# The mLSTM branch's row sums formed beside the attention branch's pairs, and three moves in the order of loads

## The chip, the cores and the metric

The kernel runs on one core of one Trainium2 chip. The metric is the device time of one execution in microseconds (us); the number to beat or miss is the median of three runs. A profiled execution gives a page and a trace, from which every duration below comes. Engines go by the names of the profile: PE is TensorE's matmul, PEld its weight load, DVE VectorE, ACT ScalarE, POOL GpSimd, SP SyncE (which issues most DMAs; SPq is its queue).

## What is computed

One layer of a hybrid decoder, for a prompt of 512 tokens and 8 samples of 4 new tokens each (544 columns, T), width 2048, all in float32:

```python
u = x @ w_in                       # q, k, v, o, z of the mLSTM; q, k, v, z of attention; two gates
h_m = mlstm(q_m, k_m, v_m, ig, lf)             # 4 heads of 512; chunked, with state C, n, m
h_a = sliding_window_attention(q_a, k_a, v_a)  # 32 heads of 64, 4 key heads, window 128, sinks
br_m = layernorm(h_m) * norm_w * sigmoid(o_m) * silu(z_m)
br_a = h_a * silu(z_a)
y = sigmoid(g_m) * (br_m @ w_proj_m) + sigmoid(g_a) * (br_a @ w_proj_a)
out = layernorm(alpha * x + y @ w_out)
```

The samples attend to a stored window of 128 keys and values each (`state_attn_k`, `state_attn_v`, 1 MB each) and update a stored mLSTM state.

## The kernel before

**Products.** Each float32 product is made of three fp32r products: an operand is split into a high part (a cast, ACT: `hilo` or `split`) and the rest (a subtraction, DVE). A *plain tile* is 128 output rows: for each of 16 blocks k of 128 inputs, three products in two halves of 272 columns, 96 matmuls of 128x272 (`gemm`, L232; `products`, L213). Its weights come in two halves (`raw`, 512 KB, by SP), each split into `wh` and `wl` of 128x1024; `wh` and `wl` have two buffers.

A *pair* (`paired`, L726) makes two output tiles with a Strassen-like scheme: seven half products of 24 matmuls instead of 192 matmuls in all. It needs sums of blocks of the activations: beside the operand itself four sums, called s1, n2, n3 and s4, which join blocks k and k+8 and the two halves of columns. Sums of the weights are formed on DVE, or by an adding DMA on POOL. A pair's weights are prepared three steps (half products) ahead.

**Stages.** First the products with `w_in`, beside which the attention runs as generators (`tick` in `products` and `paired` lets each of them go one step on); then plain tiles 0 to 5 of the attention branch's output product, beside which the four mLSTM heads run; then the two branches' products (`w_proj_a`, stage A, and `w_proj_m`, stage M), each partly in plain tiles and partly in pairs; then `w_out`.

- Stage A: eight plain tiles, three pairs, plain tiles 14 and 15. The four sums of its operand were formed earlier and stored in DRAM (`d_sa`); `stored_sums` (L1646) loads them on POOL's queue and splits them.
- Its tiles 14 and 15 run beside `branch(d_brm, ...)` (L1411), which loads the 16 blocks of the M operand on SP (`ev` and `c` buffers; `c6` has two) and splits them into `bh` and `bl`.
- Stage M: plain tiles 0 to 3, five pairs, plain tiles 14 and 15. Beside the four plain tiles runs `operand_sums` (L1616): it loads blocks k and k+8 on POOL's queue (`tx`), forms the four sums (four DVE instructions of 128x272) and splits each.

**Order.** Every engine executes its instructions in an order fixed when the kernel is built; a scheduler lays it down from the program's order, priorities (`tc.high_priority`) and ties (`tc.issue_after(x)`: not before x in the order). So an instruction that waits holds up all that stands behind it on its engine or queue.

**The samples' attention** (`sample_attention`, L953) runs late in the first stage. It loads the new keys, values and gates, then eight pieces of queries (`qraw`, L977), then the old keys (`kb`) and values (`vb`, both L982), all on SP. PE turns the old keys (L991).

**The mLSTM** (`mlstm`, L1562): for each head `decays(h)` forms a matrix `dm` of decays (one matmul, one DVE sum, ten exponentials on ACT), `values` and `keys` turn and split the operands (`kwh` is the high part of the weighted keys; L1487 multiplies with it), then `cells` does the rest.

Of the kernel before, what the change touches and what calls it, by code (L numbers as in the profile page):

```python
# [15 lines left out]
F32 = mybir.dt.float32  # L16
# [58 lines left out]
def _build(tc, nc, i, o, es):  # L75
# [106 lines left out]
    d_y = dr.tile([16, 128, T], F32, name="d_y")  # L182
    d_sa = dr.tile([8, 128, 4, SEQ - T // 2], F32, name="d_sa")
    d_ss = dr.tile([128, 4, 8, NS], F32, name="d_ss")
    d_o = dr.tile([12, 128, T], F32, name="d_o")
# [46 lines left out]
    def gemm(wv, c0, xh, xl, cols=EVEN, raws=(None, None), every=8, prio=0, before=None, parts=(1, 1),  # L232
             ps=None, behind=None):
# [12 lines left out]
        return ps  # L246
# [706 lines left out]
    def sample_attention():  # L953
# [5 lines left out]
        vas = t1.tile([32, 256], F32, name="vas")  # L959
        with tc.issue_after(state["load"].ins):  # L960
            nc.sync.dma_start(kas[:], d_ka[:, :, SEQ:T].rearrange("k p t -> p k t"))
            nc.sync.dma_start(vas[:], d_vr[SEQ:T])
            nc.sync.dma_start(gas[:], d_bra[:, :, SEQ:T].rearrange("k p t -> p k t"))
        kb = t1.tile([128, NB, 256], F32, name="kb")
# [4 lines left out]
        G.memset(En[:], 0.0)  # L969
        st = t1.tile([128, 4, NB], F32, name="sast")  # L970
        for kvh in range(KVH):
            half = slice((kvh % 2) * 64, (kvh % 2) * 64 + 64)
            if kvh % 2 == 0:
                yield
            with tc.issue_after(state["load"].ins):
                for a in range(2):
                    nc.sync.dma_start(qraw[half, kvh // 2, a::2],  # L977
                                      d_qa[kvh * 4:kvh * 4 + 4, a * 64:a * 64 + 64].rearrange("k p t -> p k t"))
        for t_, src in ((kb, i["state_attn_k"]), (vb, i["state_attn_v"])):
            yield  # L980
            with tc.issue_after(state["load"].ins):
                nc.sync.dma_start(t_[:], src.rearrange("b t k d -> t b (k d)"))  # L982
        yield
        yield
# [171 lines left out]
    def sample_prep(h, r):  # L1156
# [73 lines left out]
        for _ in range(0 if h else 2):  # L1230
            yield
        r.update(kv=load_kv(h, 0), den=den, num=num, qs=qs)

# [327 lines left out]

    def mlstm():  # L1562
        pre = {"v": load4(d_v, 0)}
        for _ in range(4):
# [80 lines left out]

    def stored_sums(to, p):  # L1646
        f, e = ([[p.tile([128, 4, 2, HT], F32R, tag="act", name=nm("sum" + n)) for _ in range(2)] for n in "hl"]
                for _ in range(2))
        to["n2"], to["s1"], to["n3"], to["s4"] = (
            (lambda q, k, t=t, j=j: t[q][k // 4][:, k % 4, j]) for t in (e, f) for j in range(2))  # L1650

        def load(n):
            t_ = two((tx.tile([128, T], F32, tag="tx", name=nm("tx")) if n % 7 < 4 else ev())[:])[:, :, 0:PC]
            j = n // 8 * 2
            G.dma_start(out=t_, in_=d_sa[n % 8][:, j:j + 2])
            return t_

        with tc.issue_after(state["head"].ins):
            ahead = [load(n) for n in range(7)]
        rim = c6t()  # L1660
        with tc.issue_after(state["load"].ins):
            nc.sync.dma_start(rim[:, 0:512], d_ss[:, 0:2].rearrange("p j k t -> p (j k t)"))

        def behind_weights(*a):
            with tc.issue_after(state["cast"].ins), tc.issue_after(state["split"].ins):
                hilo(*a)

        def columns(to_):
            src = rim[:, 0:512].rearrange("p (j k t) -> p k j t", j=2, k=8)
            for q in range(2):  # L1670
                behind_weights(src[:, q * 4:q * 4 + 4], *(t[q][:, :, :, PC:HT] for t in to_))

        for n in range(16):
            for _ in range(2 if 8 <= n < 12 else 1):
                yield
            k, t_ = n % 8, ahead.pop(0)
            to_ = e if n < 8 else f
            behind_weights(t_, *(t[k // 4][:, k % 4, :, 0:PC] for t in to_))
            if k == 4:
                columns(to_)  # L1680
                if n < 8:
                    with tc.issue_after(state["load"].ins):
                        nc.sync.dma_start(rim[:, 0:512], d_ss[:, 2:4].rearrange("p j k t -> p (j k t)"))
            if n + 7 < 16:
                ahead.append(load(n + 7))

# [31 lines left out]
    for ct in range(LEAD_A):  # L1718
        marks.append(state.get("cells"))
        with tc.issue_after(marks[ct - 1].ins) if ct > 1 and marks[ct - 1] else ExitStack():  # L1720
            plain_a(ct, every=(1, 2), prio=0 if ct else AHEAD)
    drain()
# [8 lines left out]
    SA = {}  # L1731
    sums_ = stored_sums(SA, act3)
    next(sums_)
# [10 lines left out]
    esB2.close()  # L1744
    tx = pool(esR, "txc", 2)
    bm_, bmh, bml, g_ = branch(d_brm, act3, lambda k: ev() if k % 5 < 3 else c6t(), order=(2, 3, 0, 1))
# [26 lines left out]
    drain()  # L1773
    XM = operands(bm_, M)
# [13 lines left out]

    paired([merge_pair(ct) for ct in range(4, 14, 2)], state["split"])
    state["end"] = None  # L1790
# [288 lines left out]
```

## Time and profile before

| | us |
|---|---|
| median of 3 runs (lowest, highest) | 2471.68 (2469.76, 2472.47) |
| profiled execution | 2473.6 |
| its span | 2471.8 |
| PE busy in it | 2431.3 |
| DVE, ACT, POOL busy | 1912.5, 1246.3, 526.6 |
| mean granted PE clock | 0.995 |

The span is the time from the first to the last instruction on the core; the profiled execution took 1.8 us more than its span. "Granted clock" is the share of PE's full speed that the throttle allowed. In a row of waits, `PE sm L991 <- DMA kb<-in_state_attn_k: 3.5, 1, 3.5` says that PE, at line 991 (writing a tile `sm`), waited once, for 3.5 us, for the DMA that fills `kb`. In a timeline, a row is the start, the duration, the engine, the line and what it did, and behind it in brackets the idle time before it and what ended that.

### The profile page before, as it was taken

What the parts mean: (1) busy time and instruction counts of PE and PEld (TensorE: products, weight loads), DVE (VectorE), ACT (ScalarE), POOL (GpSimd) and SP (SyncE); (2) the same over time, 40 slices, a digit from 0 to 9 for tenths busy, and PEclk for the clock granted to TensorE, in tenths of its full rate; (3) what the DMA queues carried; (4) which work ended last, traced back from release to release, by engine and by line L of the source; (5) the groups of instructions that cost most, each with busy time, mean ns of one, the idle gap of its engine ahead of it and who ended that gap; (6) DMA issues with size and microseconds to landing.
All of it is one profiled execution on the core that took longest, in us unless ns stands there. A gap on an engine that the chain in (4) does not pass through costs nothing.

```text
span 2471.8 us, 48922 instructions
## 1 busy us (share of the span) xinstructions
PE 2431.3 (98%) x19374; PEld 2374.7 (96%) x19374; DVE 1912.5 (77%) x2860; ACT 1246.3 (50%) x2064; POOL 526.6 (21%) x503
## 2 busy tenths in 40 slices
PE   9999999999999999999999999999999999999997
PEld 8999999999999998999999999999999999999997
DVE  7778888888888896887878888878755676777667
ACT  6466676676676654433433444544644444334431
POOL 4114334333334320121121122110000120110111
PEclk9999999999999999999999999999999999999998
DMA  6876666667776755578687677687754598798876
GB/s 180 201 178 158 155 163 149 161 160 164 176 178 164 172 139 135 130 229 244 183 239 241 170 235 230 178 250 216 242 165 154 177 259 255 213 228 252 214 221 193
DMA packets 568478, 479.01 MB, mean 194 GB/s; under 512 B 48313, under 2 KB 463465, under 8 KB 567993
## 3 DMA queue, kind: packets, MB, share of 16 engines
q1 hardware_dynamic: 549208, 409.30, 56.6%
q0 software_dynamic: 17840, 64.23, 13.3%
q8 instruction: 152, 2.49, 0.4%
q10 hardware_dynamic: 1200, 2.36, 0.3%
q14 instruction: 78, 0.63, 0.1%
HBM read 325.75 MB, written 100.77 MB: 173 GB/s over the span
## 4 chain that ended last, share of the span: by engine, by line
PE 85%; DMA 5%; issue 4%; DVE 3%; ACT 1%; SPq 1%; POOL 0%; DVEq 0%; POOLq 0%; ACTq 0%
PE bank L693 45%; PE bank L695 22%; PE bank L218 5%; PE sm L1487 2%; PE sm L218 1%; PE sm L1519 1%; PE sm L808 1%; PE bank L1294 1%; PE sm L1535 1%; DVE wl L209 1%; PE sm L859 1%; DMA tx<-d_brm 1%; PE sm L1945 1%; DMA VB<-d_kv 1%; PE sm L834 1%
## 5 line engine op out<-in xcount | busy, mean ns | idle before, releaser
L208 ACT CAST wh<-raw 128x1024 fp32r<-128x1024 f32 x641 | 671.6, 1048 | 819.6 <-PE bank L693 698.6
L209 DVE TENSOR_TENSOR wl<-raw,wh 128x1024 fp32r<-128x1024 f32 x641 | 800.2, 1250 | 191.0 <-ACT wh L208 164.9
L693 PE MATMUL bank<-xk,wh 128*128 128x272 f32 x2336 | 323.9, 289 | 0.0
L673 DVE TENSOR_TENSOR raw<-raw,raw 128x1024 f32<-128x1024 f32 x244 | 311.1, 1276 | 14.5 <-DMA raw<-in_w_in 8.4
L693 PEld LDWEIGHTS bank<-xk,wh 128*128 128x128 f32 x2336 | 303.4, 188 | 2.9 <-issue 2.4
L712 POOL TENSOR_TENSOR ev<-p,ev 128x272 f32<-128x272 f32 x85 | 114.4, 1346 | 483.2 <-ACT ev L711 435.4
L693 PE MATMUL bank<-n2h,wh 128*128 128x272 f32 x656 | 170.4, 292 | 2.3 <-ACT wh L208 2.3
L693 PE MATMUL bank<-s1h,wh 128*128 128x272 f32 x656 | 170.5, 292 | 0.0
L695 PE MATMUL bank<-xk,wl 128*128 128x272 f32 x1168 | 169.9, 288 | 0.0
L693 PE MATMUL bank<-n3h,wh 128*128 128x272 f32 x656 | 169.5, 291 | 0.0
L693 PE MATMUL bank<-s1l,wh 128*128 128x272 f32 x656 | 168.8, 289 | 0.0
L693 PE MATMUL bank<-n2l,wh 128*128 128x272 f32 x656 | 167.9, 287 | 0.0
L693 PE MATMUL bank<-n3l,wh 128*128 128x272 f32 x656 | 167.5, 288 | 0.0
L693 PE MATMUL bank<-s4h,wh 128*128 128x272 f32 x656 | 167.1, 288 | 0.0
L693 PE MATMUL bank<-s4l,wh 128*128 128x272 f32 x656 | 166.8, 287 | 0.0
L695 PEld LDWEIGHTS bank<-xk,wl 128*128 128x128 f32 x1168 | 155.6, 188 | 0.1
L671 POOL DMA_DIRECT2D raw<-raw x96 | 83.2, 867 | 316.6 <-DVE ev L720 200.8
L693 PE MATMUL bank<-a11h,wh 128*128 128x272 f32 x584 | 150.5, 289 | 0.0
L693 PE MATMUL bank<-a11l,wh 128*128 128x272 f32 x584 | 149.4, 288 | 0.0
L693 PEld LDWEIGHTS bank<-n2h,wh 128*128 128x128 f32 x656 | 123.5, 188 | 3.6 <-ACT wh L208 2.8
L693 PEld LDWEIGHTS bank<-s1h,wh 128*128 128x128 f32 x656 | 124.4, 190 | 1.0 <-issue 0.7
L693 PEld LDWEIGHTS bank<-n3h,wh 128*128 128x128 f32 x656 | 123.4, 188 | 1.7 <-issue 1.4
(516 smaller groups left out, 5798.5 us busy)
## 6 DMA issues: line engine op xcount, KB each, us to landing
raw<-in_w_in SPq DMA_DIRECT2D x296, 512.0 KB
raw<-raw POOLq DMA_DIRECT2D x96, 512.0 KB, 5.0
C<-in_state_mlstm_C SPq DMA_DIRECT2D x32, 1024.0 KB
out<-C SPq DMA_DIRECT2D x64, 512.0 KB
raw<-in_w_proj_a SPq DMA_DIRECT2D x32, 512.0 KB
raw<-in_w_proj_m SPq DMA_DIRECT2D x32, 512.0 KB
raw<-in_w_out SPq DMA_DIRECT2D x32, 512.0 KB
d_v<-ev SPq DMA_DIRECT2D x16, 272.0 KB
```

Of the source, the lines that this page charges most:

```text
L208: state["cast"] = A.copy(wh[:, k:k + n], raw[:, k:k + n])
L209: state["split"] = V.tensor_tensor(out=wl[:, k:k + n], in0=raw[:, k:k + n], in1=r32(wh[:, k:k + n]), op=ALU.subtract)
L218: PE.matmul(ps[f][:, :w], a[:, kk], b(k, c, w), start=(k == 0 and n == 0), stop=(k == 15 and n == 2))
L671: G.dma_start(out=w[out][:], in_=w[b][:], accum_op=ALU.add)
L673: V.tensor_tensor(out=w[out][:], in0=w[a][:], in1=w[b][:], op=ALU.add)
L693: PE.matmul(ps, wh[:, k], x(p, k), start=(first and k == 0 and p == 0), stop=False, skip_group_check=True)
L695: state["end"] = PE.matmul(ps, wl[:, k], x(0, k), start=False, stop=(k == 7), skip_group_check=True)
L712: G.tensor_tensor(out=c22, in0=p1, in1=c11, op=ALU.subtract)
L808: PE.matmul(pp[:, c0 + w0:c0 + 256], qs[a][:, j * 128:j * 128 + 128], kx[:, k0:k0 + 256 - w0], start=(n == 0), stop=(n == 1))
L834: PE.transpose(pt[:, b * 128:b * 128 + 128], s_[:, b, 128:256], ident)
L859: PE.matmul(po[:, b * 128:b * 128 + n], VA[:, b], p_[:, 2 * b:2 * b + n // 128], start=(b == 0 and m == 0), stop=(b == 3 and m == 1), skip ...
L1487: state["cells"] = PE.matmul(pp[:, 0:258], a[:, b * 128:b * 128 + 128], b_[:, b, f], start=(b == 0 and n == 0), stop=(b == 3 and n == 2))
```

## The change

Four things, of which the first two belong together:

1. *The mLSTM branch's sums are formed earlier and stored.* A new generator, `row_sums`, runs beside stage A's three pairs and its tail: for each k of 0 to 7 it loads blocks k and k+8 on POOL's queue (into `ms` and a `c6` buffer), forms the four sums with `branch_sums` on DVE, and stores them on SP into a new DRAM tile `d_sm` (128x1088, 557 KB each). Stage M then takes its sums through `stored_sums`, which now serves both branches: 16 loads of 128x544 on POOL's queue (five `tx` buffers), and 16 splits of 128x544 instead of 32 of 128x272.
2. *Stage M has two plain tiles ahead of its pairs, not four*, and six pairs, not five.
3. *The samples' old keys are loaded first* in `sample_attention`; the eight pieces of `qraw` go to POOL's queue, and the old values are loaded two steps later.
4. *Smaller moves*: the first head's `decays` start at the mLSTM's first load; a head's `keys` come before the split of the same block; `load_kv` is tied to the last weight load; and the second half of plain tile 5 of stage A is placed behind the last head's products (`hold`).

```diff
@@ gemm
-            products(ps, half, wh, wl, xh, xl, cols, every[half] if isinstance(every, tuple) else every)
+            with tc.issue_after(state["cells"].ins) if hold and half else ExitStack():
+                products(ps, half, wh, wl, xh, xl, cols, every[half] if isinstance(every, tuple) else every)
@@ sample_attention
         with tc.issue_after(state["load"].ins):
+            nc.sync.dma_start(kb[:], i["state_attn_k"].rearrange("b t k d -> t b (k d)"))
             nc.sync.dma_start(kas[:], d_ka[:, :, SEQ:T].rearrange("k p t -> p k t"))
...
-            with tc.issue_after(state["load"].ins):
-                for a in range(2):
-                    nc.sync.dma_start(qraw[half, kvh // 2, a::2],
-                                      d_qa[kvh * 4:kvh * 4 + 4, a * 64:a * 64 + 64].rearrange("k p t -> p k t"))
-        for t_, src in ((kb, i["state_attn_k"]), (vb, i["state_attn_v"])):
-            yield
-            with tc.issue_after(state["load"].ins):
-                nc.sync.dma_start(t_[:], src.rearrange("b t k d -> t b (k d)"))
-        yield
+            for a in range(2):
+                G.dma_start(out=qraw[half, kvh // 2, a::2],
+                            in_=d_qa[kvh * 4:kvh * 4 + 4, a * 64:a * 64 + 64].rearrange("k p t -> p k t"))
+            yield
+            if kvh == 1:
+                with tc.issue_after(state["load"].ins):
+                    nc.sync.dma_start(vb[:], i["state_attn_v"].rearrange("b t k d -> t b (k d)"))
@@ mlstm
+        spawn(decays(0))
         pre = {"v": load4(d_v, 0)}
...
-            spawn(decays(h))
+            if h:
+                spawn(decays(h))
...
-                two_parts(kts[c], (kh, kl))
                 n_ = keys(h, c, kts[c])
                 next(n_)
+                two_parts(kts[c], (kh, kl))
@@ new
+    def row_sums(src, dst):
+        while sums_ in live:
+            yield
+        esB2.close()
+        ms = pool(esM, "ms", 2)
+
+        def load(k):
+            t_, o_ = ms.tile([128, 4, HT], F32, tag="ms", name=nm("ms")), c6t()
+            G.dma_start(out=t_[:, 0:4:2], in_=src[k].rearrange("p (c x) -> p c x", c=2))
+            G.dma_start(out=o_[:], in_=src[k + 8])
+            return t_, o_
+
+        ahead = [load(0), load(1)]
+        for k in range(8):
+            for _ in range(2):
+                yield
+            t_, o_ = ahead.pop(0)
+            with tc.issue_after(state["split"].ins):
+                for _ in branch_sums(t_[:], o_[:, 0:HT], o_[:, HT:T], dst[k]):
+                    pass
+            if k < 6:
+                ahead.append(load(k + 2))
@@ stage A
+    esM = ExitStack()
+    spawn(row_sums(d_brm, d_sm))
     paired([pair_a(ct) for ct in range(PAIR_A, TAIL_A, 2)], state["split"], rest=sums_)
...
-    tx = pool(esR, "txc", 2)
+    tx = pool(esR, "txc", 5)
@@ stage M
-    spawn(operand_sums(d_brm, M, act))
-    for ct in range(4):
+    sums_ = stored_sums(M, act, d_sm)
+    next(sums_)
+    spawn(sums_)
+    for ct in range(2):
         merge = merged(ct, plain=True)
-        sg = merge([p_[:, :HT] for p_ in gemm(wm, ct * 128, bmh, bml, every=4, prio=AHEAD)])
+        sg = merge([p_[:, :HT] for p_ in gemm(wm, ct * 128, bmh, bml, every=2, prio=AHEAD)])
...
-    paired([merge_pair(ct) for ct in range(4, 14, 2)], state["split"])
+    paired([merge_pair(ct) for ct in range(2, 14, 2)], state["split"], rest=sums_)
```

How the change moves instructions. In what follows each block is a run of one engine's rows; the number behind a tile's name is the build's count. The lines of the changed kernel lie a little further down (L991 is L990 there, L977 stays, L218 is L219, L209 is L210, L254 is L256, L1696 is L1729).

SP's queue at the samples' attention, before:

```order
L879 DMA d_sa<-s_11208 512x1x240
L195 DMA raw_11508<-in_w_in 128x8x128
L961 DMA kas<-d_ka 128x2x32
L962 DMA vas<-d_vr 32x256
L963 DMA gas<-d_bra 128x16x32
L977 DMA qraw<-d_qa 64x4x32 x8
L982 DMA kb<-in_state_attn_k 128x8x256
L982 DMA vb<-in_state_attn_v 128x8x256
```

and in the changed kernel:

```order
L881 DMA d_sa<-s_11209 512x1x240
L196 DMA raw_11509<-in_w_in 128x8x128
L970 DMA kb<-in_state_attn_k 128x8x256
L971 DMA kas<-d_ka 128x2x32
L972 DMA vas<-d_vr 32x256
L973 DMA gas<-d_bra 128x16x32
L982 DMA vb<-in_state_attn_v 128x8x256
```

The load of `kb` has moved from behind eleven small loads to directly behind the weights.

PE at the turning of the old keys, before (`a11h` is the first half product of a pair, `s4h` the sixth):

```order
L695 MATMUL bank_11710<-a11h_114,wl_11579 128x272 x4
L991 MATMUL sm_11568<-cc,kb 128x128 x2
L991 MATMUL sm_11573<-cc,kb 128x128 x2
L695 MATMUL bank_11710<-a11h_114,wl_11579 128x272 x4
L693 MATMUL bank_11772<-s1h_648,wh_11641 128x272
```

and in the changed kernel:

```order
L697 MATMUL bank_11441<-s4h_723,wl_11504 128x272 x3
L990 MATMUL sm_11536<-cc,kb 128x128 x2
L990 MATMUL sm_11541<-cc,kb 128x128 x2
L697 MATMUL bank_11441<-s4h_723,wl_11504 128x272 x5
L695 MATMUL bank_11477<-xk_7_119,wh_11546 128x272
```

The first four transposes stand in the sixth half product of the pair before, not in the first of the next: five products' matmuls, a whole half product and twenty more earlier.

DVE at the end of stage A, around the merge of its tile 15 (L1696, L1729), before; `bl` is the M operand, `s1l` to `s4l` its sums:

```order
L254 TENSOR_TENSOR bl_24968<-c_3425_25244,bh_24967 128x544
L209 TENSOR_TENSOR wl_25276<-raw_25273,wh_25275 128x1024
L254 TENSOR_TENSOR n2l_25370<-tx_25303,n2h_25369 128x272
L254 TENSOR_TENSOR n2l_25370<-tx_25305,n2h_25369 128x272
L254 TENSOR_TENSOR bl_24968<-ev_25212,bh_24967 128x544
L254 TENSOR_TENSOR n3l_25374<-tx_25303,n3h_25373 128x272
L254 TENSOR_TENSOR n3l_25374<-tx_25305,n3h_25373 128x272
L254 TENSOR_TENSOR bl_24968<-ev_25260,bh_24967 128x544
L1696 TENSOR_TENSOR c_3410_25120<-bank_25122,c_3410_25120 128x272
L1696 TENSOR_TENSOR c_3410_25120<-bank_25123,c_3410_25120 128x272
L209 TENSOR_TENSOR wl_25334<-raw_25331,wh_25333 128x1024
```

and in the changed kernel (`ms` is the last row sum):

```order
L879 TENSOR_TENSOR ms_24878<-ms_24878 128x272
L1729 TENSOR_TENSOR c_3426_25197<-bank_25199,c_3426_25197 128x272
L1729 TENSOR_TENSOR c_3426_25197<-bank_25200,c_3426_25197 128x272
L880 TENSOR_TENSOR ms_24878<-c_3391_24879,ms_24878 128x272
L210 TENSOR_TENSOR wl_25441<-raw_25438,wh_25440 128x1024
L256 TENSOR_TENSOR bl_25047<-c_3418_25120,bh_25046 128x544
L256 TENSOR_TENSOR bl_25049<-ev_25158,bh_25048 128x544
L256 TENSOR_TENSOR bl_25049<-ev_25174,bh_25048 128x544
L256 TENSOR_TENSOR bl_25049<-ev_25190,bh_25048 128x544
L256 TENSOR_TENSOR bl_25049<-c_3422_25142,bh_25048 128x544
L256 TENSOR_TENSOR bl_25043<-c_3432_25219,bh_25042 128x544
L256 TENSOR_TENSOR suml_25346<-tx_25352,sumh_25344 128x544
```

Before, the last `bl` stood ahead of the merge of tile 15. Now thirteen of the sixteen stand behind it, the last one 24 rows further down, with eight stored sums and two `wl` among them.

SP's queue at the same place in the changed kernel (`c_3422`, `c_3433` and `c_3441` take turns in one `c6` buffer, which `c_3391`, the last row sum's second block, held before them):

```order
L1422 DMA c_3418_25120<-d_brm 128x544
L1730 DMA d_t<-c_3426_25197 128x544
L881 DMA d_sm<-ms_24878 128x1088
L1422 DMA c_3422_25142<-d_brm 128x544
L196 DMA raw_25644<-in_w_proj_m 128x8x128
L1791 DMA c_3507_25737<-d_sgm 128x544
L1422 DMA c_3432_25219<-d_brm 128x544
L1422 DMA ev_25251<-d_brm 128x544
L1422 DMA ev_25267<-d_brm 128x544
L1422 DMA ev_25289<-d_brm 128x544
L1422 DMA c_3433_25235<-d_brm 128x544
L1422 DMA c_3440_25305<-d_brm 128x544
```

Ten of the sixteen loads of the operand stand here, around the store of tile 15's result (L1730); before, all sixteen stood ahead of that store.

More of the change, by code (lines that the diff above doesn't have):

```diff
@@ L1644, in operands, with stored_sums, four @@
         return [side_by_side(tiles, 0), s1, n2, side_by_side(low, 0), n3, s4, side_by_side(low, HT)]
[L1646 to L1648 removed]
+    def stored_sums(to, p, src, rim=None, behind=None):
+        width = PC if rim else HT
+        def four():
+            return [[p.tile([128, 4, 2, HT], F32R, tag="act", name=nm("sum" + n)) for _ in range(2)] for n in "hl"]
+        f = four() if rim else None
+        e = four()
+        f = f or four()
         to["n2"], to["s1"], to["n3"], to["s4"] = (
             (lambda q, k, t=t, j=j: t[q][k // 4][:, k % 4, j]) for t in (e, f) for j in range(2))
+        turn, own = (7, 4) if rim else (5, 5)
         def load(n):
[L1653 removed]
+            t_ = two((tx.tile([128, T], F32, tag="tx", name=nm("tx")) if n % turn < own else ev())[:])[:, :, 0:width]
             j = n // 8 * 2
[L1655 removed]
+            G.dma_start(out=t_, in_=src[n % 8][:, j:j + 2])
             return t_
[L1658 to L1662, printed above, removed]
+        with tc.issue_after(behind.ins) if behind else ExitStack():
+            ahead = [load(n) for n in range(turn)]
+        if rim:
+            edge = c6t()
+            with tc.issue_after(state["load"].ins):
+                nc.sync.dma_start(edge[:, 0:512], rim[:, 0:2].rearrange("p j k t -> p (j k t)"))
         def behind_weights(*a):
@@ L1731, in _build @@
     SA = {}
-    sums_ = stored_sums(SA, act3)
+    sums_ = stored_sums(SA, act3, d_sa, d_ss, state["head"])
     next(sums_)
```

34 lines of the change are left out of this document (17 added, 17 removed).

## The prediction

> **What bounds the kernel now.** I read the page's first part, then the waits of TensorE, then the stretches of the two stages that the change touches, and last the timelines at the waits themselves. All times are in us. First the page, then the waits (engine, line, what it waited for: total, times, longest):
>
> ```profile
> PE 2431.3 (98%) x19374; PEld 2374.7 (96%) x19374; DVE 1912.5 (77%) x2860; ACT 1246.3 (50%) x2064; POOL 526.6 (21%) x503
> ```
> ```profile
> PE sm L1487 <- ACT kwh L253: 5.4, 3, 4.3
> PE sm L991 <- DMA kb<-in_state_attn_k: 3.5, 1, 3.5
> ...
> PE bank L218 <- DVE wl L209: 3.2, 3, 1.4
> PE bank L693 <- ACT wh L208: 2.3, 2, 1.7
> PE sm L336 <- DMA xr<-in_x_prompt: 2.2, 1, 2.2
> PE sm L1535 <- ACT t L1118: 0.9, 1, 0.9
> ```
> TensorE is busy for 98%: matmuls set the time, and all its waits together are some 25 us. So an edit gains only by fewer matmuls, by a wait of this list that goes, or by clock that isn't lost. The stretches (length, PE busy, weight loads, DVE, ACT, POOL, granted clock, DMA share, GB/s):
>
> ```profile
> 931.00:950.00 19.00, 15.51 (x181) 15.00 (x180) 10.50 (x14) 8.03 (x14) 2.73 (x2) 0.82 0.80 232
> ...
> 2010.00:2073.00 63.00, 63.00 (x505) 62.91 (x504) 43.12 (x57) 26.30 (x34) 7.71 (x8) 1.00 0.88 236
> 2073.00:2097.00 24.00, 24.00 (x195) 24.00 (x194) 15.01 (x25) 11.29 (x21) 1.51 (x2) 1.00 0.94 294
> 2097.00:2146.00 49.00, 46.55 (x368) 45.89 (x367) 37.44 (x73) 20.32 (x36) 6.04 (x7) 1.00 0.74 217
> 2146.00:2250.00 104.00, 104.00 (x834) 104.00 (x833) 69.78 (x92) 39.92 (x48) 13.19 (x13) 1.00 0.89 234
> ```
> Two things stand here. A matmul of 128x272 costs 104.00/834 = 0.1247 where nothing waits. And the merge stages (from 2010 on) keep the DMA engines at 0.88 to 0.94: TensorE is the bound there, and the DMA engines are close behind it.
>
> **The samples' old keys.** TensorE around 931, and what SyncE's queue issued before:
>
> ```profile
> 930.28 0.29 PE L693 MATMUL bank<-a11l,wh 128*128 128x272 f32 x1
> 930.40 0.66 PE L695 MATMUL bank<-a11h,wl 128*128 128x272 f32 x4
> 934.56 1.09 PE L991 MATMUL sm<-cc,kb 128*128 128x128 f32 x4 [3.50 <-DMA kb<-in_state_attn_k]
> 935.29 1.25 PE L695 MATMUL bank<-a11h,wl 128*128 128x272 f32 x4
> 936.35 0.43 PE L693 MATMUL bank<-s1h,wh 128*128 128x272 f32 x1
> ```
> ```profile
> 918.33 0.37 SPq L195 DMA_DIRECT2D raw<-in_w_in  x1
> ...
> 920.35 8.12 SPq L977 DMA_DIRECT2D qraw<-d_qa x8
> 928.52 0.60 SPq L982 DMA_DIRECT2D kb<-in_state_attn_k  x1
> ```
> The wait costs twice: 3.50 idle, and a clock of 0.82 over the 19 us after it, which is 0.18 x 19 = 3.4 of lost work (a matmul shows 0.43 instead of 0.29). The load of kb is late because SyncE spends 8.12 on eight small loads ahead of it; it then takes 934.56 - 928.52 = 6.0. In the new order kb stands right behind the weights of 918.33: issued at 918.8, there at 924.8, or 926.5 if the 0.5 MB of weights ahead of it come first. TensorE too comes earlier: the transposes move ahead by 5 + 24 + 20 = 49 matmuls (rest of one product, a whole one, 20 of the next), 6.1, so to 931.06 - 6.1 = 924.9. The new wait is 0 to 1.6, I take 1.0: a gain of 2.5 and of the 3.4 of clock. Ends: 0, if kb is as late as now, and 6.9. I take -5.9. The eight loads on POOL's queue (0.73 each by the row of L1655 below, 5.9 together) are wanted only for the scores behind kb; nothing is queued behind them there that TensorE needs within 8 us, so they cost 0, at most the 1.6 of a wait like the one above. The clock: waits of 2.2 (L336, though at the start) and 1.7 (L693) show no halved matmuls behind them, 3.5 and 4.3 do, so a wait of 1.0 should cost none. The Trainium skill (TensorE: Matmul & The Clock Gate, section What's actually happening) has the clock back after one busy window of about 3.4 us, which makes 1.7 of a halving; by it the gain here would be 1.7 smaller and the sum below that much higher. The row of 931 to 950 shows twice that, and I go by the row.
>
> **Decays at the first load.** The largest wait, 4.3 at L1487, is that of the first mLSTM head. ScalarE before it:
>
> ```profile
> 1772.80 0.62 ACT L253 CAST t<-t 128x512 fp32r<-128x512 f32 x1 [1.10 <-DMA t<-d_q]
> ...
> 1776.74 1.28 ACT L1507 ACT_TABLE_LOAD   x1
> ...
> 1780.20 1.86 ACT L1507 ACTIVATE dm<-f,colT 128x128 f32<-128x128 f32 x6
> 1781.97 0.60 ACT L253 CAST t<-t 128x512 fp32r<-128x512 f32 x1
> 1782.47 0.62 ACT L253 CAST kwh<-f 128x512 fp32r<-128x512 f32 x1
> ```
> ```profile
> 1783.23 0.64 PE L1487 MATMUL sm<-vh,kwh 128*128 128x258 f32 x2 [4.31 <-ACT kwh L253]
> ...
> 1785.19 0.43 PE L218 MATMUL bank<-bl,wh 128*128 128x272 f32 x1
> ...
> 1786.91 0.28 PE L218 MATMUL bank<-bh,wh 128*128 128x272 f32 x1
> ```
> ScalarE works without a break from 1773 on, and kwh comes last. The change moves the first decays' matmul and their DVE sum earlier, but in ScalarE's order the table load and all ten dm still stand directly ahead of kwh, and in the same order. So I take 0, between 0 and the whole 4.3 + 1.7 (half pace from 1783.2 to 1786.8). `hold` shifts half a plain tile behind the last head's products; the waits there are at most the 0.9 of L1535: 0, within 0.9 either way.
>
> **Fewer matmuls.** Two plain tiles (2 x 96) become one pair (7 x 24 = 168): 24 x 0.1247 = -3.0.
>
> **The sums of the mLSTM branch.** Two waits of the M stage were tied to forming them there:
>
> ```profile
> 2104.68 0.52 PE L218 MATMUL bank<-bh,wl 128*128 128x272 f32 x2 [1.39 <-DVE wl L209]
> 2117.98 0.52 PE L218 MATMUL bank<-bh,wl 128*128 128x272 f32 x2 [1.00 <-DVE wl L209]
> ```
> The weights' wl stood on DVE behind sums that waited for tx. These go: -2.4. But something else becomes late. Rows of DVE at the end of attention tile 15 (I call that moment T), one SyncE load and its use, and a run of four conversions:
>
> ```profile
> 2085.81 0.73 DVE L254 TENSOR_TENSOR bl<-ev,bh 128x544 fp32r<-128x544 f32 x1 [0.55 <-ACT bh L253]
> 2086.45 0.78 DVE L1696 TENSOR_TENSOR c<-bank,c 128x272 f32<-128x272 f32 x2
> 2087.15 1.22 DVE L209 TENSOR_TENSOR wl<-raw,wh 128x1024 fp32r<-128x1024 f32 x1
> ```
> ```profile
> 2080.28 0.38 SPq L1422 DMA_DIRECT2D ev<-d_brm  x1
> ```
> ```profile
> 2085.13 0.65 ACT L253 CAST bh<-ev 128x544 fp32r<-128x544 f32 x1 [2.39 <-DMA ev<-d_brm]
> ```
> ```profile
> 1769.65 2.62 DVE L254 TENSOR_TENSOR bl<-pf,bh 128x544 fp32r<-128x544 f32 x4
> ```
> Before, all 16 conversions of the M operand are ahead of tile 15's merge (L1696), so M tile 0 finds them. In the new order 13 of 16 stand behind it (now L1729), with 8 conversions of stored sums and two wl among them: DVE alone needs 0.78 + 0.39 + 2 x 1.22 + 21 x 0.655 = 17.4 from T on for what M tile 0 wants within 96 x 0.1247 = 12.0. With the last two k's (1.5) tile 0 then ends at T + 18.9: 6.9 late. That is the lower end. The loads make it longer. Rows of the attention branch's stored sums (the same two queues), the last one the time from issue to landing:
>
> ```profile
> L1655 POOL DMA_DIRECT2D tx<-d_sa x10: 722/734/832, 1928.1 to 1994.0; - x10
> L879 SPq DMA_DIRECT2D d_sa<-s x8: 549/550/606, 588.2 to 915.9; - x8
> ...
> DMA to landing us min/median/max: 6.1/7.7/9.8
> ```
> First chain: k = 4, 9 and 14 share one c6 buffer with the last row sum, which is free at T + 1.2; the SyncE store ahead takes 0.55; a link is 2085.13 - 2080.28 = 4.85 of transfer, 0.65 and 0.73 of conversion, 0.4 of issue: 8.0, 14.6, 21.2, and the tile ends at T + 22.7, 10.7 late. Second chain, on POOL: the second load of d_sm takes the memory of the last stored sum, so it waits for that store (T + 1.2 + 4.85 = 6.05), lands 6.1 later and is converted at 13.5; DVE then has k = 11, a wl and the third sum (2.5, 16.0); the eighth load takes the third's buffer: 6.1 + 1.4, 23.5; k = 14 stands behind it on DVE: 24.2, and the tile ends at 25.7, 13.7 late. With the median 7.7 it is 16.9. I take 13.7, as the least landing that those rows show, and the ends 6.9 and 16.9. The waits at k = 4 and k = 14 are over 3.5, so the clock is lost too: in the middle the next wait covers it, after the last one 1.7 as at 1783. DVE and the loads are later free, so tile 1 and the first pair pay nothing.
>
> **The traffic.** d_sm adds a store and a load of 8 x 128 x 1088 x 4 bytes, 8.9 MB, at the 294 of a full stretch 30 of all the engines. Free between 2010 and 2146 are 0.12 x 63 + 0.06 x 24 + 0.26 x 49 = 21.7. It doesn't fit; 8 go over, most of it into the 13.7 above. Weights are prepared three steps (9 us) ahead, which covers the rest but a wait or so: +1.0, ends 0 and 8. The row sums themselves are 32 instructions of 128x272 at 0.39 (half of L1696's 0.78), 12.5 of DVE in a stretch where it is busy for 43 of 63: 0.
>
> **The sum.** -5.9 - 3.0 - 2.4 + 0 + 0 + 13.7 + 1.7 + 1.0 = +5.1. The profiled execution took 2473.6 (span 2471.8 and 1.8 around it), 1.9 above the median of the three runs, 2471.68. So the profiled time becomes 2478.7, and the median 2476.8; I say 2477. About 0.2% (4.9 us) is what a measurement can tell from no change.
>
> **Rivals.**
> *The transfers aren't late (faster).* If every load takes its own time alone, kb is there at 924.8, before TensorE at 924.9 (-6.9), and M tile 0 is late by DVE's 6.9 alone, with no wait in it that reaches 3.5: -6.9 - 3.0 - 2.4 + 6.9 = -5.4, 2466.3. For it: six of the operand's loads go to buffers that are free early, and three conversions stay ahead of T. Against: three links in a row, and 0.94 of DMA. It decides where tile 0 is late by less than 7.4: 0.27, of which 0.2 over 0.2% faster.
>
> *The DMA engines become the bound.* The 8 us don't fall into the wait but make the attention pairs' weights late: +5.1 + 7 gives 2483.8; 0.12. The Trainium skill (DMA: Bandwidth & Descriptors, section Issuing engines are not separate DMA queues) says that transfers of all queues share the same 16 engines, and by that POOL's queue hides nothing; no row of before shows it.
>
> *The old keys aren't earlier.* If kb waits on SyncE for the store ahead of it, 3.5 and the clock stay: +5.1 + 5.9 gives 2482.7; 0.07.
>
> *Decays first does what it says*, and the 4.3 and 1.7 go: 2476.8 - 6.0 = 2470.8, or 2466 if tile 0 is late by the first chain's 10.7 alone and loses no clock; 0.08, of which 0.05 faster.
>
> *My forecast* (tile 0 late by 10 to 17): 0.46, its own range 2473 to 2481, and 0.24 of it over the 0.2%.
>
> Over all: faster 0.25, same 0.32 (0.07, 0.03 and 0.22), slower 0.43 (0.24, 0.12 and 0.07). The range for 8 in 10 goes from 2463 (the first rival with a part of the first head's wait gone) to 2486 (the DMA bound with its full 8).
>
> **What would show it.** Right: no wait over 2 at kb and a clock of 1.00 after it; no waits of L219 for wl at M tiles 1 and 2; in M tile 0 two to four waits for bh or bl, 10 to 17 together, with matmuls of 0.43 behind the last; the 4.3 at L1487 as before. Wrong: M tile 0 without waits over 2, a first head without its wait, or waits for wh or wl within the attention pairs.

## The result and the profile after

The changed kernel takes 2502.51 us (median of 4 runs, 2500.24 to 2504.87) where the kernel before took 2472.07: slower by 1.2%, ratio 1.0121 (95% interval 1.0103 to 1.0139). The prediction said 2477. The mechanism that it built its number on is there, and with what goes with it the merge stage makes up half of the loss; the other half lies in moves that it had put at nothing or not counted at all.

The profiled execution has a span of 2503.1, 31.3 above that of before. Of the page, TensorE's busy time:

```profile
PE 2443.9 (98%) x19350; PEld 2383.9 (95%) x19350; DVE 1918.0 (77%) x2853; ACT 1246.4 (50%) x2052; POOL 548.7 (22%) x538
```

The 24 matmuls fewer are there (19350 for 19374), and yet TensorE was busy for 12.6 us more: matmuls at a halved clock take longer (0.43 for 0.29 in the rows). The waits of TensorE in the changed kernel (total, times, longest):

```profile
PE sm L1299 <- DMA VB<-d_kv: 11.4, 3, 5.7
PE bank L219 <- ACT bh L255: 6.5, 3, 5.3
PE sm L1487 <- issue: 3.4, 1, 3.4
...
PE sm L1487 <- ACT kwh L255: 3.2, 3, 2.6
PE sm L990 <- DMA kb<-in_state_attn_k: 3.0, 1, 3.0
PE bank L695 <- ACT wh L209: 2.7, 2, 2.3
```

The largest is new: VB, an operand of the samples' mLSTM state update (before: 0.5 at TensorE). The stretches around the waits, in the changed kernel (length, PE, weight loads, DVE, ACT, POOL, granted clock, DMA share, GB/s):

```profile
931.00:950.00 19.00, 19.00 (x189) 18.51 (x188) 12.71 (x17) 7.70 (x14) 2.99 (x2) 0.91 0.64 180
1040.00:1080.00 40.00, 34.31 (x262) 32.33 (x261) 27.27 (x39) 17.07 (x25) 10.39 (x14) 0.91 0.65 189
1240.00:1260.00 20.00, 16.93 (x124) 15.62 (x123) 11.52 (x14) 5.84 (x7) 0.77 (x1) 0.91 0.82 227
1595.00:1615.00 20.00, 17.38 (x128) 16.08 (x127) 12.66 (x14) 6.35 (x8) 1.70 (x3) 0.91 0.74 183
1945.00:1960.00 15.00, 12.18 (x77) 11.54 (x75) 12.23 (x21) 7.34 (x15) 0.00 (x0) 0.77 0.76 253
2106.00:2130.00 24.00, 17.41 (x102) 15.91 (x101) 16.17 (x26) 11.24 (x18) 5.37 (x10) 0.79 1.05 355
```

All but the first of them have no lost clock in the kernel before; its row for the same place as the second:

```profile
1040.00:1080.00 40.00, 37.72 (x301) 35.54 (x301) 31.79 (x42) 19.29 (x27) 13.69 (x13) 1.00 0.66 185
```

Clock lost is worked out as length times what is missing of 1.00. An account of the 31 from the two traces (waits and lost clock of the changed kernel, less what stood at the same place before):

| where | us |
|---|---|
| VB at three places: waits 11.4 - 0.5, clock 3.6 + 1.8 + 1.8 | +18.1 |
| later mLSTM heads: waits 3.2 - 1.1 (5.4 - 4.3), clock 3.4 (at 1945) | +5.5 |
| stage M's first tile: waits 6.5, clock 5.0 (at 2106); weights in the last attention pair just ahead of it 2.3 | +13.8 |
| clock at the start (0.96 over 0 to 40) and near the end (0.89 over 2455 to 2470) | +3.2 |
| 24 matmuls fewer | -3.0 |
| the two waits for wl in stage M, gone | -2.4 |
| waits for wh in the first stage, gone (2.3 before) | -2.3 |
| the old keys: 3.5 + 3.4 became 3.0 + 1.7 | -2.2 |
| the first mLSTM head: 4.3 became 3.4 | -0.9 |
| sum | +29.8 |

The rest is spread over small waits. This is the account of one execution of each kernel, that of the changed one the slowest of its four; the runs below price some of the parts otherwise.

The old keys, on SyncE's queue and at TensorE:

```profile
920.91 0.37 SPq L196 DMA_DIRECT2D raw<-in_w_in  x1
921.90 0.37 SPq L970 DMA_DIRECT2D kb<-in_state_attn_k  x1
```
```profile
930.30 0.63 PE L990 MATMUL sm<-cc,kb 128*128 128x128 f32 x4 [2.97 <-DMA kb<-in_state_attn_k]
```

Issued at 921.9 and not at 918.8, and 8.4 us on its way instead of 6.0.

### The profile page after: what moved, and what is told of

Its sections match the earlier page's. It is cut to its first block, busy times and chain, and to the rows that moved or that the text cites. A ratio compares the mean times of both kernels' runs of the same rounds, so it can differ in the third digit from the quotient of the medians.

```text
span 2503.1 us, 48963 instructions
## 1 busy us (share of the span) xinstructions
PE 2443.9 (98%) x19350; PEld 2383.9 (95%) x19350; DVE 1918.0 (77%) x2853; ACT 1246.4 (50%) x2052; POOL 548.7 (22%) x538
## 4 chain that ended last, share of the span: by engine, by line
PE 88%; DMA 7%; DVE 3%; issue 2%; ACT 1%; SPq 0%; POOL 0%; DVEq 0%; POOLq 0%; ACTq 0%
PE bank L695 46%; PE bank L697 23%; PE bank L219 5%; PE sm L1487 2%; PE sm L1519 1%; PE sm L810 1%; PE sm L1535 1%; PE bank L1294 1%; PE sm L861 1%; PE sm L219 1%; DMA VB<-d_kv 1%; DMA c<-d_brm 1%; PE sm L1981 1%; DMA tx<-d_y 1%; DVE wl L210 1%
## 5 line engine op out<-in xcount | busy, mean ns | idle before, releaser
L209 ACT CAST wh<-raw 128x1024 fp32r<-128x1024 f32 x644 | 674.9, 1048 | 864.5 <-PE bank L695 712.5
L210 DVE TENSOR_TENSOR wl<-raw,wh 128x1024 fp32r<-128x1024 f32 x644 | 803.9, 1249 | 202.6 <-ACT wh L209 166.3
L675 DVE TENSOR_TENSOR raw<-raw,raw 128x1024 f32<-128x1024 f32 x246 | 312.9, 1272 | 13.7 <-DMA raw<-in_w_proj_a 6.5
L695 PE MATMUL bank<-n2h,wh 128*128 128x272 f32 x616 | 161.5, 293 | 0.0
L695 PE MATMUL bank<-s1h,wh 128*128 128x272 f32 x616 | 159.1, 291 | 0.0
L695 PE MATMUL bank<-n3h,wh 128*128 128x272 f32 x616 | 159.0, 290 | 0.1
L695 PE MATMUL bank<-n2l,wh 128*128 128x272 f32 x616 | 159.1, 289 | 0.0
L695 PE MATMUL bank<-s4h,wh 128*128 128x272 f32 x616 | 158.5, 290 | 0.0
L695 PE MATMUL bank<-s4l,wh 128*128 128x272 f32 x616 | 158.1, 288 | 0.0
L695 PE MATMUL bank<-n3l,wh 128*128 128x272 f32 x616 | 157.4, 288 | 0.0
L695 PE MATMUL bank<-s1l,wh 128*128 128x272 f32 x616 | 157.0, 287 | 0.0
L695 PEld LDWEIGHTS bank<-s4h,wh 128*128 128x128 f32 x616 | 116.8, 190 | 1.3 <-issue 1.2
L695 PEld LDWEIGHTS bank<-s4l,wh 128*128 128x128 f32 x616 | 117.2, 190 | 0.0
```

Source lines behind the costliest of these rows:

```text
L209: state["cast"] = A.copy(wh[:, k:k + n], raw[:, k:k + n])
L210: state["split"] = V.tensor_tensor(out=wl[:, k:k + n], in0=raw[:, k:k + n], in1=r32(wh[:, k:k + n]), op=ALU.subtract)
L675: V.tensor_tensor(out=w[out][:], in0=w[a][:], in1=w[b][:], op=ALU.add)
L695: PE.matmul(ps, wh[:, k], x(p, k), start=(first and k == 0 and p == 0), stop=False, skip_group_check=True)
```

## The experiments

Three parts of the change can be built alone: the samples' moves, the mLSTM's moves and the merge stage's part. The runs are told by what they settle. Ratios are to the kernel before, with their 95% intervals; the medians of that kernel in the four sets of runs were 2471.34, 2472.10, 2471.54 and 2471.68.

### Which part costs

*The merge part alone* (row sums, stored sums, two plain tiles fewer; all else as before):

> The kernel before with the merge stage's part alone (row sums beside the attention pairs, stored, two plain tiles fewer in stage M); the samples and the mLSTM as before. Theory: stage M's tile 0 starved of its operand, as in the changed kernel (waits 7 us with the clock halved for 10 us, 2.3 for weights in the last attention pair), against 3.0 and 2.4 saved: 2472 + 5 to + 10, so 2477 to 2482. Rival (what is lost there comes from the shift of everything by the samples' waits, not from the part itself): 2472 - 5 = 2467.

Measured: 2487.23, 1.0065 (1.0050 to 1.0080): +15.9. The waits of stage M's first tile are there with nothing shifted ahead of them (7.0, and 5.2 of clock: 0.80 over 2084 to 2110), so they come from the part itself; it costs more than I had put down.

*Everything but the merge part:*

> The changed kernel with the merge stage as before (operand sums in stage M, four plain tiles): old keys first, decays first, hold and the tie stay. Theory: the waits for VB with their clock (+18) and the longer wait in the fourth mLSTM head (+5) less 2 at the old keys remain: 2472 + 18 to + 22, so 2490 to 2494. Rival (the merge part is what costs): 2472 or less.

Measured: 2486.29, 1.0060 (1.0045 to 1.0075): +15.0, less than I had expected from the trace. 15.9 and 15.0 add up to the 31 of the changed kernel: by these times neither half makes the other dearer or cheaper.

### VB: one step fewer, or the tie?

The change drops one of the six steps (`yield`) of the samples' attention, and ties a head's first load of KB and VB to the last weight load. TensorE's order shows that all the samples' later work stands 24 matmuls earlier, one half product or 3.0 us. In the trace, TensorE and SyncE at the first such place of the changed kernel:

```profile
1056.33 1.07 PE L1294 MATMUL bank<-C,qz 128*32 128x512 f32 x8
1063.09 0.80 PE L1299 MATMUL sm<-VB,Ab 32*128 32x512 f32 x4 [5.69 <-DMA VB<-d_kv]
1063.82 0.59 PE L695 MATMUL bank<-s4h,wh 128*128 128x272 f32 x1
1064.21 0.43 PE L695 MATMUL bank<-s4l,wh 128*128 128x272 f32 x1
```
```profile
1049.95 2.56 SPq L1140 DMA_DIRECT2D d_kv<-qcl  x4
...
1056.12 0.54 SPq L1147 DMA_DIRECT2D VB<-d_kv  x1
```

VB is stored to DRAM (d_kv) and loaded back in another layout; the load waits for the store, and TensorE goes on with VB 7.0 after the load's issue. In the kernel before:

```profile
1053.69 0.55 SPq L1148 DMA_DIRECT2D VB<-d_kv  x1
```
```profile
1061.10 0.50 PE L1299 MATMUL sm<-VB,Ab 32*128 32x512 f32 x4 [0.47 <-DMA VB<-d_kv]
```

There was no slack in that way at this place before either: TensorE came 0.5 before VB. The 5.7 are that 0.5, the 3.2 by which TensorE now comes earlier (1057.4 for 1060.6), and the 2.0 by which VB now comes later (1063.09 for 1061.10): its load stands at 1056.12 on SyncE's queue and not at 1053.69. At the other two places the waits are 3.1 and 2.6, where TensorE had not waited before. Two runs take the causes apart. The step put back, with the keys still first:

```diff
                     nc.sync.dma_start(vb[:], ...)
         yield
+        yield
```

> The changed kernel with one more step (yield) in the samples' attention, so that all later work of the samples stands where it stood before in TensorE's order (24 matmuls later), while the old keys stay first. Theory A (the missing step: the samples' heads want VB 3.0 us earlier than its way through DRAM allows): the three waits of L1299 for VB, 11.4 us, and the three halvings of the clock behind them, 6.8, go nearly whole: about 2502.5 - 17 = 2485. Theory B (the tie of the load of KB and VB to the last weight load holds VB up): the waits stay, about 2502.

Measured: 2492.21, 1.0084 (1.0069 to 1.0099), 10.3 under the changed kernel. VB's waits at TensorE, and the same stretch:

```profile
PE sm L1300 <- DMA VB<-d_kv: 0.3, 1, 0.3
```
```profile
1040.00:1080.00 40.00, 38.36 (x308) 35.89 (x310) 31.11 (x41) 19.04 (x27) 14.17 (x13) 1.00 0.71 202
```

The waits (but for 0.3) and the halved clock went at all three places, and VB's first load goes at 1051.78: the earlier TensorE and the later load both came with the missing step. The time fell by less than the 18 of the account, since stage M's first tile lost more in this run (waits of 9.8 for bh instead of 6.5, and 7.0 of clock instead of 5.0: 0.83 over 2084 to 2125). The two profiled executions are 13.8 apart (2504.87 and 2491.07), the medians 10.3.

```diff
-        with tc.issue_after(state["load"].ins):
-            r.update(kv=load_kv(h, 0), den=den, num=num, qs=qs)
+        r.update(kv=load_kv(h, 0), den=den, num=num, qs=qs)
```

> The changed kernel without the tie of a head's first KB and VB load to the last weight load. Theory A (missing step): the waits for VB stay, within 2 us of 2502.5. Theory B (the tie): they go, about 2485.

Measured: 2503.03, as the changed kernel; VB's waits are 11.7. The tie does nothing; the missing step does it.

### The old keys, and the mLSTM's moves

*Old keys first, alone, with six steps:*

> The kernel before with the samples' part alone, and with the step it dropped put back: old keys first on SyncE, the eight pieces of queries on POOL's queue, old values after them. Theory (kb still comes 2.9 us late, since TensorE wants it 49 matmuls earlier, but a wait of 2.9 doesn't always halve the clock): 2471.3 less 0.6 of wait and 0 to 3.4 of clock, so 2467 to 2471. Rival (kb earlier costs other loads): 2473 or more.

Measured: 2469.98, 0.9989 (0.9980 to 0.9998): -2.1. A gain, at the small end; the interval only just leaves out 1.

*The mLSTM's moves alone:*

> The kernel before with the mLSTM's moves alone: first head's decays at the first load, keys ahead of the split of the same block, half of plain tile 5 behind the last head's products (hold). Theory: the first head's wait goes on (3.4 to 4.3), and the fourth head's wait of 2.6 with the clock halved for 6.8 behind it, seen in the changed kernel, comes from these moves: 2471.3 + 4 to + 6, so 2475 to 2477. Rival (the fourth head's wait comes from the samples running a step early): 2470 to 2472.

Measured: 2477.21, 1.0018 (1.0007 to 1.0028): +5.1. The first head's wait is still 4.3, and the fourth head shows the new one. TensorE there:

```profile
1932.35 0.60 PE L1475 MATMUL sm<-cc,t 128*128 128x128 f32 x4
1935.53 0.75 PE L1488 MATMUL sm<-vh,kwh 128*128 128x258 f32 x2 [2.57 <-ACT kwh L254]
```

and in the kernel before, where the stretch from 1936.65 to 1940.72 is filled by 32 matmuls of plain tile 5, 4.0 us:

```profile
1936.29 0.60 PE L1474 MATMUL sm<-cc,t 128*128 128x128 f32 x4
1940.72 0.40 PE L1487 MATMUL sm<-vh,kwh 128*128 128x258 f32 x2
```

*The same without `hold`* (the split of the tile's second half stays free of the last head's products):

```diff
-            plain_a(ct, every=(1, 2), prio=0 if ct else AHEAD, hold=ct == LEAD_A - 1)
+            plain_a(ct, every=(1, 2), prio=0 if ct else AHEAD)
```

> The mLSTM's moves without hold: first head's decays at the first load, keys ahead of the split; half of plain tile 5 stays among the fourth head's products. Theory (hold takes away the 48 matmuls, 6 us, that lay between the turning of the fourth head's keys and their use, and so uncovers ScalarE's casts): the wait of 2.6 and the halved clock there go, 2472 within 1.5. Rival (the order of keys and split does it): 2476 to 2477 as with hold.

Measured: 2472.04, 1.0002 (0.9993 to 1.0010). The waits at the keys' use:

```profile
PE sm L1487 <- issue: 4.3, 1, 4.3
...
PE sm L1487 <- ACT kwh L253: 0.6, 2, 0.5
```

So `hold` is the whole 5: it takes away the matmuls under which ScalarE made kwh. The other two moves, the first head's decays at the first load and the keys ahead of the split, give nothing: the first head's 4.3 stays (the profile now names no releaser for it).

### The merge part: what makes the operand late

Stage M's first tile in the changed kernel. T, the end of attention tile 15, is 2106.7. DVE, SyncE's queue and ScalarE:

```profile
2103.61 0.44 DVE L877 TENSOR_TENSOR ms<-c,ms 128x272 f32<-128x272 f32 x1 [1.26 <-DMA ms<-d_brm]
...
2106.71 0.78 DVE L1729 TENSOR_TENSOR c<-bank,c 128x272 f32<-128x272 f32 x2
2107.41 0.43 DVE L880 TENSOR_TENSOR ms<-c,ms 128x272 f32<-128x272 f32 x1
2107.76 1.22 DVE L210 TENSOR_TENSOR wl<-raw,wh 128x1024 fp32r<-128x1024 f32 x1
2113.79 0.73 DVE L256 TENSOR_TENSOR bl<-c,bh 128x544 fp32r<-128x544 f32 x1 [4.82 <-ACT bh L255]
```
```profile
2105.96 1.83 SPq L881 DMA_DIRECT2D d_sm<-ms  x1
2107.96 0.34 SPq L1422 DMA_DIRECT2D c<-d_brm  x1
```
```profile
2113.12 0.64 ACT L255 CAST bh<-c 128x544 fp32r<-128x544 f32 x1 [6.05 <-DMA c<-d_brm]
```

The fourth block of the operand is loaded only at 2107.96, behind the store of the seventh row sum, whose second block held its buffer; that is one link earlier than I had begun the chain. The seventh sum itself was formed only from 2103.6 on, when its load had come. Why so late? Six runs on the merge part:

*No row sums* (stage M loads blocks of the branch, of the same size, in place of the sums; loading, forming and storing the sums beside stage A are left out):

```diff
-    spawn(row_sums(d_brm, d_sm))
...
-            G.dma_start(out=t_, in_=src[n % 8][:, j:j + 2])
+            G.dma_start(out=t_, in_=src[n % 8][:, j:j + 2] if rim else two(src[n]))
```

> The kernel before with stage M's stored sums, two plain tiles fewer and six pairs, but without the row sums beside the attention pairs: stage M loads, in their place, blocks of the branch itself of the same size (so its sums are the blocks, not sums of them; the forming and the store of the sums are left out). Theory A (forming the sums, with its two-buffer chain of load, sum and store, holds up the operand): 2471.3 - 5.4 = 2466. Theory B (stage M's own loads on POOL's queue and the shorter run of plain tiles do it): 2480 or more.

Measured: 2468.05, 0.9987 (0.9977 to 0.9996). Stage M with its 16 loads and two plain tiles is faster than before; all the loss, 19, comes with the row sums beside the attention branch: their loads, their forming and their store.

*The operand through other buffers* (`lambda k: ev()` for `lambda k: ev() if k % 5 < 3 else c6t()`):

> The merge part alone (2487.2) with all sixteen blocks of the operand through the three ev buffers, none through the c6 buffers that the row sums hold. Theory A (the shared buffers make the operand late): the waits of stage M's tile 0, 7 with 5 of lost clock, fall under 3: 2487.2 - 9 = 2478. Theory B (traffic, or the order on DVE, makes it late whatever the buffer): 2484 or more.

Measured: 2484.59, 1.0050 (1.0032 to 1.0068): 2.6 less (bh 4.6 instead of 7.0), though the single times overlap (2480.14 to 2487.62, and 2485.35 to 2489.55 through the shared buffers). So the shared buffers, the first of my two chains, are a small part.

*Sums formed, not stored:*

> The merge part alone (2487.2) with the row sums formed but not stored; stage M loads blocks of the branch of the same size in place of the stored sums (so its sums are the blocks). Theory A (the store is the long link: the two ms buffers are free for the next load only when their store has landed, 5.7 to 8.7 us in the changed kernel): the row sums end ahead of tile 15, tile 0's waits fall under 3, 2472 within 4. Theory B (loads of the blocks and DVE's work are enough to hold up the operand): 2482 or more.

Measured: 2475.29, 1.0011 (1.0002 to 1.0020). So 12 of the 19 go with the store, and 7 (2475.29 against 2468.05) with loading and forming the sums. The scheduler lays the order anew in each of these kernels: with the whole store POOL issues two loads of the second blocks (c) and then two into ms, without it the two kinds in turn; what the store does and what this order does is not parted. POOL's loads into the two ms buffers, with the whole store (the merge part alone): the first of eight, some of those between, the last:

```profile
2010.94 0.75 POOL L1704 DMA_DIRECT2D ms<-d_brm  x1 [1.99 <-DVE suml L255]
...
2038.97 0.72 POOL L1704 DMA_DIRECT2D ms<-d_brm  x1 [6.42 <-DMA d_sm<-ms]
...
2061.79 0.72 POOL L1704 DMA_DIRECT2D ms<-d_brm  x1 [4.88 <-DMA d_sm<-ms]
...
2079.62 0.71 POOL L1704 DMA_DIRECT2D ms<-d_brm  x1 [6.08 <-DMA d_sm<-ms]
...
2081.80 0.72 POOL L1704 DMA_DIRECT2D ms<-d_brm  x1 [1.47 <-DMA d_sm<-ms]
```

and without a store, the first and the last:

```profile
2007.64 0.75 POOL L1705 DMA_DIRECT2D ms<-d_brm  x1 [2.04 <-DVE suml L255]
...
2055.21 0.72 POOL L1705 DMA_DIRECT2D ms<-d_brm  x1 [3.95 <-DVE ms L879]
```

With the store the eight loads spread over 71 us, a round of two every 23.6; without it over 48, a round every 15.9. The loads wait for the store to land before a buffer is theirs.

*Is it the tie, or the bytes?* The store kept and tied to the buffer, but small (16 columns, 8 KB), and half (279 KB). Both hold only what the first three of a row sum's four DVE instructions make, so they can go one instruction earlier than the whole; stage M again loads blocks of the branch:

```diff
+                nc.sync.dma_start(dst[k][:, 0, 0:16], t_[:, 0, 0:16])
```

> The merge part alone, each row sum stored with 16 columns only (8 KB instead of 557), in the same place and tied to the same buffer; stage M loads blocks of the branch in place of the sums (so its sums are the blocks). Without a store it took 2475.3, with the whole store 2487.2. Theory A (the bytes): as without a store, 2475 within 3. Theory B (the tie: a buffer is free only when its store has landed, whatever its size): 2484 or more.

> As the one before with half of each row sum stored (279 KB). Theory A (the bytes): half way, 2479 to 2483. Theory B (the tie): 2484 or more.

Measured: 2482.17 (1.0043, 1.0027 to 1.0059) and 2486.45 (1.0058, 1.0041 to 1.0075). The half store fits the tie; the small one lies between the two theories. Of the 12, the tie with next to no bytes is 7; half the bytes bring it to 11, and the whole store to 12 (these last two can't be told apart: 2483.67 to 2488.26, and 2485.35 to 2489.55). In the small store's trace POOL still waits up to 7.7 us for it: the store has to come to the head of SyncE's queue, and land. That store is issued at 2057.09, and POOL's load behind it at 2062.07: 5.0 for 8 KB.

TensorE's waits with the half store show something else:

```profile
PE bank L694 <- ACT wh L209: 5.5, 5, 1.6
...
PE bank L219 <- ACT wh L209: 4.0, 2, 3.3
...
PE bank L696 <- DVE wl L210: 2.3, 1, 2.3
...
PE bank L219 <- ACT bh L254: 0.9, 1, 0.9
```

The operand is hardly late any more (bh 0.9, with the whole store 7.0), and yet the time is the same: now the weights are late, by 10.0 in all between 1985 and 2150, where the whole store has 3.7. So the late operand is one form that the loss takes, and late weights are another. Whether the transfers crowd each other, or the stores hold up what stands behind them on SyncE's queue, no run here parts.

*A quicker generator* (one step for each row sum instead of two, with the operand in ev):

> The merge part alone with the operand through the ev buffers (2484.6) and one step for each row sum instead of two. Theory A (the chain load, sum, store is bound by its transfers and two buffers, not by its steps): the row sums end where they did, 2482 to 2488. Theory B (the steps set its pace): they end some 20 us earlier, tile 0 finds its operand, 2470 or less, which would beat the kernel before.

Measured: 2493.01, 1.0087 (1.0073 to 1.0101): 8 slower than with two steps, which neither theory had. Its eight loads into ms spread over 73.6 us (2007.20 to 2080.77), as long as with two steps (2012.32 to 2085.89 through ev): the steps weren't what held the sums back. Its largest wait is 12.1 (seven times) for wh, 4.3 of it in the attention pairs and 5.6 in stage M's first pair. Why the weights come later than with two steps isn't shown.

### What is better than both

*Old keys first with six steps, and the mLSTM's moves without `hold`:*

> The kernel before with the old keys first (with the step put back) and the mLSTM's two moves without hold. Theory: the keys' gain of 2 stays and the mLSTM's moves give nothing either way: 2470 to 2471, 1 to 2 under the kernel before. Rival (the first head's wait falls from 4.3 to 3.4 as in the changed kernel, and the clock with it): 2468.

Measured: 2468.79, 0.9988 (0.9979 to 0.9997), as good as the keys alone (2469.98). This is the part of the change worth keeping, some 2 to 3 us, with an interval that only just leaves out 1.

## Why the prediction was wrong

- **Outside its range, by a term that wasn't there.** The sum had no term for what the missing step moves. I had counted the 49 matmuls by which the keys' transposes stand earlier, as a gain, and didn't ask what else of that generator moves with them: all the samples' mLSTM, 24 matmuls earlier, against a way through DRAM that at its first place had 0.5 us too little already. The row of TensorE's waits for VB (0.5) stood in the view I read; the step's size is in the order. That is 10.3 by the run, 18 by the account of the traces.
- **`hold`, put at "0, within 0.9 either way"**, failed: +5. I priced it by the waits that stood at the end of the heads and not by what the moved matmuls had covered: 32 of them, 4.0 us, lay on the fourth head's casts.
- **The row sums themselves, put at 0** because VectorE had idle time for them, failed too: loaded and formed but not stored, they cost 7 (2475.29 against 2468.05). Their loads, which now stand beside the attention pairs, had no term either. By which wait is not settled; in that run's profile the largest between 1985 and 2150 is 2.3.
- **Decays at the first load: 0.** Right: the first head's wait stays.
- **The old keys: -5.9.** The right sign, mis-sized: the runs show -2.1. The load is issued 3.1 later than I put it (the weights ahead of it were themselves issued 2.6 later) and takes 8.4 instead of 6.0; the wait is 3.0, not 1.0.
- **24 matmuls, -3.0, and the two waits, -2.4.** About right: without the row sums the merge part gives -4.
- **Stage M's operand: +13.7 and 1.7 of clock.** The mechanism was right (the operand stands behind T, and tile 0 waits for bh with the clock halved after it), and the total is near: 6.5 to 9.8 of waits and 5.0 to 7.0 of clock. In part that is luck, since the waits are shorter than the 10 to 17 of the forecast and the lost clock is three to four times as long. The lateness began a block earlier than I put it, at the fourth. Of the chains, the shared c6 buffers were worth 2.6; of the store's 12, 7 stay when its bytes are taken away and the tie to the ms buffers is kept. I used the store's transfer once, at the chain's end (T + 6.05); it acts on every round of two sums from the second on.
- **Traffic: +1.0, ends 0 and 8.** Too small: the merge part costs 15.9 where the terms for it (-3.0, -2.4, 13.7, 1.7 and 1.0) sum to 11.0. Weights were late in the attention pairs (2.7 in the merge part alone, nothing before), which the prediction had named as a sign that it is wrong. The Trainium skill (DMA: Bandwidth & Descriptors, section Issuing engines are not separate DMA queues) says that transfers of all queues run on the same 16 engines; no run here isolates that. A high share of busy DMA engines alone didn't make weights late: over 2073 to 2097 it was 1.04 without the row sums and 1.05 with the quick generator, and TensorE was busy for all 24 us in both.
- **The rivals.** None of them gives what was measured. "Old keys not earlier" came nearest at its place, and the late weights of "the DMA engines become the bound" are there, whatever makes them late.

By the runs, the step's 10.3, the mLSTM's 5.1, the keys' -2.1 and the merge part's 15.9 add up to 29 of the 30 by which the medians differ.

## What to carry to other kernels

When a generator loses or gains a step, everything behind that step moves on every engine; look up what it does behind the place you care for, above all round trips through memory. A small wait there says that there is no slack; no wait doesn't say how much there is. Before matmuls are moved away, ask what ran under them. A stage that loads, sums and stores through two buffers runs at the pace of the whole round, store and queue included: reckon its time as rounds times that, and compare it with the stretch it is to fit in, before pricing what it delays.

## What the runs showed of the hardware

The same wait costs different amounts of clock. The stretch 925 to 950 in four kernels, all with one wait for kb (2.9, 2.9, 3.1, 3.4): the merge part without row sums, the change without the merge part, the keys alone, the merge part alone:

```profile
925.00:950.00 25.00, 22.08 (x254) 21.39 (x254) 16.96 (x22) 10.88 (x19) 3.00 (x2) 1.00 0.76 208
```
```profile
925.00:950.00 25.00, 22.07 (x204) 21.40 (x203) 15.79 (x19) 9.10 (x15) 2.98 (x2) 0.86 0.67 184
```
```profile
925.00:950.00 25.00, 21.86 (x229) 21.04 (x231) 15.66 (x20) 9.69 (x16) 2.98 (x2) 0.93 0.65 176
```
```profile
925.00:950.00 25.00, 21.63 (x203) 20.99 (x201) 14.39 (x19) 9.44 (x16) 2.72 (x2) 0.86 0.66 182
```

The missing share of 25 us is 0, 3.5, 1.7 and 3.5: nothing, twice, once and twice 1.7, after waits that differ by half a microsecond, and with 2.9 at both ends. The Trainium skill (TensorE: Matmul & The Clock Gate, section What's actually happening) has the clock watched in windows of about 3.4 us that run free of the kernel; steps of 1.7 (3.4 at half pace) fit that, though a wait of 2.9 is shorter than such a window, and the double loss isn't in it; here the measurement decides. A wait of 3.5 shows the same: in the kernel before, the prediction's rows have 3.4 of clock lost behind it, and in the run of the mLSTM's moves alone the wait is 3.5 and the clock 1.00 over 925 to 950. Whatever decides it, I could not have read it from one execution: a wait of about 3 us has to be priced with 0 to 3.5 of clock on top.
